# Attention steps of a hybrid trunk layer: five steps an item, three units between scores and transposes, and three norm sums two units later

## The chip, the cores and the metric

One Trainium2 chip, one core. The metric is the time of the kernel on the device in microseconds; the profile beside it shows one execution. PE is TensorE (with PEld for its weight loads), DVE VectorE, ACT ScalarE, SP the engine that issues most DMAs.

## The reference

One layer on h = [16 meta tokens; 512 tokens], width 1024, in float32:

```python
h = h + 0.5 * swiglu(rmsnorm(h, ffn1_norm), w_gate, w_up, w_down)
z = rmsnorm(h, mix_norm) @ w_in
y_rwkv = rwkv7_mix(z[..., :RWKV_COLS], ...)        # 8 heads x 64, state over tokens
y_attn = swa_sink_attention(z[..., RWKV_COLS:] + b_attn, sinks)   # 8 q / 2 kv heads x 64
h = h + concat([y_rwkv, y_attn]) @ w_out
h = h + 0.5 * swiglu(rmsnorm(h, ffn2_norm), ...)
return rmsnorm(h, final_norm)[:, 16:]
```

Attention is causal by chunks of 64 tokens: the queries of a chunk see the 16 meta tokens, their own chunk and the two before it, with a distance penalty and a sink in the softmax:

```python
s = einsum(q, k) * scale - slope * distance      # window and meta columns
p = softmax(concat([sink, s_meta, s_window]))
o = p_meta @ v_meta + p_window @ v_window
```

## The kernel before

The tokens are worked in two halves, hf 0 (272 with the meta tokens) and hf 1 (256). All large products run over weight *units* of 128 x 1024 weights: SP loads `raw`, ACT casts it to `whi` (L124), DVE makes `wlo` = raw − whi (L127), and PE does 24 matmuls of 256 or 272 columns (three products: hi·hi, hi·lo, lo·hi). `drive` walks a list of some 320 units: FFN 1 of both halves, W_in of half 0, W_out of half 0, W_in of half 1, FFN 2 of half 0 with W_out of half 1 in it, FFN 2 of half 1.

Beside the units run two *sides*, which are generators: `rwkv` (`tinv`, the inverse of triangular 32 x 32 blocks in 31 DVE steps L731/L733, closed by DMAs issued on ACT, L739 to L751; then `chain` over the chunks) and `attention`. After each unit `advance` gives each side one step, up to its next `yield UNIT_END`. So a `yield` is a distance of one unit in the program. The order of each engine's instructions is then set by a scheduler with priorities (the chain's instructions rank before their place in the program), so that work of a step can move by a unit or two. Each engine runs its instructions in that order.

In a step of the chain, X1 (L819, L821), X2 (L834) and X3 (L843, L844) are products on PE; between them ACT and DVE copy operands (`Rs` L824, `UV` L836), `values` makes the next chunk's operands in a pair of PSUM banks called `as` (L797, L802; copies L805, L806), and `group_norm` takes sums (L876), a root (L878, with a table load on ACT) and a reciprocal (L879). Attention uses the same single pair `as`. Each half has 4 chunks (`ci`) with 2 *items* (`mp2`, each two query heads on both kv heads), 8 items a half, counted here 1 to 16. An item: scores on PE (L914), maxima on DVE (L920 to L924), exp on ACT with a table load (L927), reciprocals (L929) and scaling (L930), transposes on PE (L935, L937), copies `pT` (L942, L944), products with the values (L947, L950), output as hi and lo parts (L955, L956). Once for each chunk the values are transposed into `VK` (L904 to L908).

Norms: `last(hf)` starts the sum of squares on PE (L315), root and reciprocal (L319, L320) and the split in hi and lo (L345 to L347) of the next layer part's operand. It is called by `drive` from a list `late`: an entry (n, g) waits for n further units before g runs.

Of the kernel before, what the change touches and what calls it, by code (L numbers as in the profile page):

```python
# [37 lines left out]
UNIT_END = -1.0  # L38
# [32 lines left out]
class Prog:  # L71
# [23 lines left out]
    def t(self, pool, shape, tag, dt=F32, bufs=1):  # L95
        return pool.tile(shape, dt, name=self.nm(tag), tag=tag, bufs=bufs)
# [372 lines left out]
    def w_out(self, hf, mo, last):  # L469
        c0 = RO[hf]  # L470

        def f(d):
            def f_(w):
                ps = self.bank()
                self.mm3([ps[:, :256]], w, [lambda k: mo[k // 4][:, k % 4]], 8, WO)
                r = self.res[hf, d][:, c0:TT[hf]]
                self.V.tensor_tensor(out=r, in0=ps[:, :256], in1=r, op=ALU.add)
                self.sq_acc(hf, d, c0)
                if d == NK - 1:
                    self.late.append((0, lambda: last(hf)))  # L480
            return f_

        return [(("o", d), 8, self.cost((hf,), 8), f(d)) for d in range(NK)]
# [405 lines left out]
    def attention(self, hf, st, mo, ap_):  # L889
        A, V, P, PE, t = self.A, self.V, self.P, self.PE, self.t  # L890
        for ci in range(4):
            c = 4 * hf + ci
            nw = min(c + 1, 3)
            W = 17 + 64 * nw
            if c < 3:
                KC, VC = self.KT[:, 0:W], self.VT[:, 0:W]
            else:
                KC, VC = t(ap_, [128, 209], "KC"), t(ap_, [128, 209], "VC")
                for dst, src in ((KC, self.KT), (VC, self.VT)):
                    P.tensor_copy(out=dst[:, 0:17], in_=src[:, 0:17])  # L900
                    P.tensor_copy(out=dst[:, 17:], in_=src[:, 17 + 64 * (c - 2):17 + 64 * (c + 1)])
            VK = t(ap_, [128, 2, 128], "VK")
            b = self.banks()[0]
            PE.transpose(b[0:81, 0:128], VC[:, 0:81], self.ident)  # L904
            if nw > 1:
                PE.transpose(b[0:W - 81, 128:256], VC[:, 81:W], self.ident)
                A.copy(out=VK[0:W - 81, 1], in_=b[0:W - 81, 128:256])
            A.copy(out=VK[0:81, 0], in_=b[0:81, 0:128])  # L908
            yield UNIT_END
            kss = (slice(0, 64), slice(64, 128))  # L910
            for mp2 in range(2):
                bs, rows = self.banks(), []
                for b, ks in zip(bs, kss):
                    PE.matmul(b[:, 0:W], st["Q"][ks, ci, 2 * mp2:2 * mp2 + 2, :].rearrange("p m t -> p (m t)"), KC[ks, 0:W],  # L914
                              start=True, stop=True)
                for kv in range(2):
                    g, x = 2 * kv + mp2, bs[kv][:, 0:W]
                    s = t(ap_, [128, 209], "s", bufs=2)
                    m = t(ap_, [128, 4], "m", bufs=4)
                    V.tensor_tensor_reduce(out=s[:, 0:17], in0=x[:, 0:17], in1=self.tabm[:, g, c], scale=1.0, scalar=-3e38,  # L920
                                           op0=ALU.add, op1=ALU.max, accum_out=m[:, 0:1])
                    V.tensor_tensor_reduce(out=s[:, 17:W], in0=x[:, 17:W], in1=self.tabw[:, g, 192 - 64 * nw:], scale=1.0,
                                           scalar=-3e38, op0=ALU.add, op1=ALU.max, accum_out=m[:, 1:2])
                    V.tensor_scalar(out=m[:, 2:3], in0=m[:, 0:1], scalar1=m[:, 1:2], scalar2=-1.0, op0=ALU.max, op1=ALU.mult)  # L924
                    rows.append((s, m))
                for s, m in rows:
                    A.activation(s[:, 0:W], s[:, 0:W], AF.Exp, bias=m[:, 2:3], accum_out=m[:, 3:4])  # L927
                for s, m in rows:
                    V.reciprocal(m[:, 3:4], m[:, 3:4])  # L929
                    A.activation(s[:, 0:W], s[:, 0:W], AF.Copy, scale=m[:, 3:4])  # L930
                yield UNIT_END
                yield UNIT_END
                b, bo = self.banks()
                for kv, (s, m) in enumerate(rows):
                    PE.transpose(b[0:81, 256 * kv:256 * kv + 128], s[:, 0:81], self.ident)  # L935
                    if nw > 1:
                        PE.transpose(b[0:W - 81, 256 * kv + 128:256 * kv + 256], s[:, 81:W], self.ident)  # L937
                yield UNIT_END
                pTs = []
                for kv in range(2):  # L940
                    pT = t(ap_, [128, 2, 128], "pT", bufs=2)
                    A.copy(out=pT[0:81, 0], in_=b[0:81, 256 * kv:256 * kv + 128])  # L942
                    if nw > 1:
                        A.copy(out=pT[0:W - 81, 1], in_=b[0:W - 81, 256 * kv + 128:256 * kv + 256])  # L944
                    pTs.append(pT)
                for kv, ks in enumerate(kss):
                    PE.matmul(bo[ks, 0:128], VK[0:81, 0, ks], pTs[kv][0:81, 0], start=True, stop=(nw == 1))  # L947
                if nw > 1:
                    for kv, ks in enumerate(kss):
                        PE.matmul(bo[ks, 0:128], VK[0:W - 81, 1, ks], pTs[kv][0:W - 81, 1], start=False, stop=True)  # L950
                yield UNIT_END
                ms, ts = slice(2 * mp2, 2 * mp2 + 2), slice(64 * ci, 64 * ci + 64)
                ov = bo[:, 0:128].rearrange("p (m t) -> p m t", m=2)
                mh, ml = mo[1][:, ms, 0, ts], mo[1][:, ms, 1, ts]
                A.copy(out=mh, in_=ov)  # L955
                V.tensor_tensor(out=ml, in0=ov, in1=mh.bitcast(F32), op=ALU.subtract)  # L956
                yield UNIT_END


def program(tc, io, out):  # L960
    with ExitStack() as ctx:
        pr = Prog(ctx, tc, io)
        n = {}
        A, B, AB = (0,), (1,), (0, 1)
# [6 lines left out]
        def final(hf):  # L971
# [6 lines left out]
            for d in (0, 1, 2, 3, 6, 7, 4, 5):  # L978
# [6 lines left out]
                if d % 2:  # L985
# [1 line left out]

        gu = lambda f, g, hfs: pr.ffn_gu(f, g, hfs, n)
        dn = lambda f, g, hfs, last=None: pr.ffn_down(f, g, hfs, last, last is final and hfs == B,
                                                           6 if last is final and hfs == A else 0)  # L990
        act = lambda fn: [(None, 0, 0, fn)]
        pools = {}

# [215 lines left out]
```

## Time and the profile before

| what | value |
|---|---|
| median of 3 runs | 1140.03 us (1139.44 to 1143.7) |
| the profiled execution | 1143.3 us, its span 1140.5 us |
| PE busy | 1084.7 us, 95% |
| DVE busy | 826.8 us, 72% |
| ACT busy | 674.6 us, 59% |

The span runs from the first to the last instruction that the profiler saw; the time of the same execution holds 2.8 us more. Busy shares are means over the whole span, whose stages have different limits.

### The profile page before, as it was taken

The page shows a single profiled execution, that of the slowest core. Times are in us where ns is not written, and L with a number is a line of the kernel's source. Part 1 is how long each engine was busy: PE and PEld are TensorE (multiplying, and loading weights), DVE is VectorE, ACT ScalarE, POOL GpSimd, SP SyncE. Part 2 cuts the span into 40 slices and gives each one's busy share as a digit, 9 for nine tenths or more (in the row PEclk, how much of TensorE's full clock was granted, in tenths as well). Part 3 has the DMA queues.
Part 4 walks back from the last instruction along what each step waited for, and adds up shares of the span by engine and source line. Part 5 has one row for each costly group of instructions (what it writes and reads, how often), then busy time and mean ns, then how long its engine had stood idle before and what let it go on. Part 6 is the DMA issues. An engine that isn't in the chain of part 4 may idle for free.

```text
span 1140.5 us, 23845 instructions
## 1 busy us (share of the span) xinstructions
PE 1084.7 (95%) x9621; PEld 1022.1 (90%) x9621; DVE 826.8 (72%) x1533; ACT 674.6 (59%) x1166; POOL 31.6 (3%) x91
## 2 busy tenths in 40 slices
PE   8999999999999997989999998998999899999996
PEld 7999999998899997878989898997888898888884
DVE  7866666777778994466888776995676488776666
ACT  7545454676667634676667685563667477545453
POOL 0000000021000000000001000000000000000000
PEclk8999999999999998999999998997999899999998
DMA  7565655544336546222655445546225356666661
GB/s 267 181 183 170 202 171 166 184 146 152 126 115 198 173 147 172 95 66 86 182 152 169 144 137 164 153 145 188 76 76 167 108 158 201 212 209 187 188 193 60
DMA packets 68722, 178.82 MB, mean 157 GB/s; under 512 B 21620, under 2 KB 26868, under 8 KB 68612
## 3 DMA queue, kind: packets, MB, share of 16 engines
q1 hardware_dynamic: 52384, 173.70, 49.5%
q10 hardware_dynamic: 16228, 3.61, 1.5%
q8 instruction: 75, 1.23, 0.4%
q14 instruction: 35, 0.29, 0.1%
HBM read 173.54 MB, written 3.74 MB: 155 GB/s over the span
## 4 chain that ended last, share of the span: by engine, by line
PE 79%; DVE 8%; ACT 6%; DMA 3%; issue 3%; ACTq 1%; DVEq 0%; SPq 0%
PE big L218 19%; PE big L219 18%; PE big L200 13%; PE big L206 11%; PE big L208 5%; PE big L227 5%; DVE wlo L127 2%; ACT whi L124 2%; DVE tmp L731 2%; DVE rn L733 1%; DMA zk<-d 1%; ACT s L927 1%; PE as L914 1%; DMA d<-rn 1%; ACT L927 1%
## 5 line engine op out<-in xcount | busy, mean ns | idle before, releaser
L124 ACT CAST whi<-raw 128x1024 fp32r<-128x1024 f32 (+1 forms) x321 | 334.5, 1044 | 289.8 <-PE big L219 150.1
L127 DVE TENSOR_TENSOR wlo<-raw,whi 128x1024 fp32r<-128x1024 f32 x320 | 389.5, 1218 | 112.6 <-ACT whi L124 93.4
L218 PE MATMUL big<-n0a,whi 128*128 128x272 f32 (+1 forms) x464 | 124.0, 296 | 10.0 <-ACT whi L124 5.7
L219 PE MATMUL big<-h,whi 128*128 128x256 f32 (+1 forms) x528 | 133.0, 285 | 0.0
L218 PE MATMUL big<-h,whi 128*128 128x256 f32 (+1 forms) x528 | 130.8, 286 | 1.4 <-ACT whi L124 1.4
L219 PE MATMUL big<-n0a,whi 128*128 128x272 f32 (+1 forms) x464 | 122.4, 292 | 0.4 <-DVE n0a L347 0.3
L218 PE MATMUL big<-n0b,whi 128*128 128x272 f32 (+1 forms) x464 | 121.7, 293 | 0.8 <-ACT n0b L955 0.4
L219 PE MATMUL big<-n0b,whi 128*128 128x272 f32 (+1 forms) x464 | 121.3, 291 | 0.4 <-DVE n0b L347 0.4
L218 PEld LDWEIGHTS big<-h,whi 128*128 128x128 f32 x528 | 98.5, 189 | 2.8 <-ACT whi L124 1.6
L218 PEld LDWEIGHTS big<-n0a,whi 128*128 128x128 f32 x464 | 89.8, 194 | 12.1 <-ACT whi L124 6.8
L219 PEld LDWEIGHTS big<-h,whi 128*128 128x128 f32 x528 | 99.3, 189 | 1.3 <-issue 0.9
L219 PEld LDWEIGHTS big<-n0a,whi 128*128 128x128 f32 x464 | 90.1, 194 | 1.8 <-DVE n0a L347 0.9
L218 PEld LDWEIGHTS big<-n0b,whi 128*128 128x128 f32 x464 | 89.4, 194 | 2.3 <-ACT n0b L346 0.9
L219 PEld LDWEIGHTS big<-n0b,whi 128*128 128x128 f32 x464 | 89.3, 193 | 1.4 <-DVE n0b L347 0.7
L218 PE MATMUL big<-n1a,whi 128*128 128x256 f32 x288 | 76.6, 295 | 6.9 <-ACT whi L124 6.3
L227 PE MATMUL big<-h,wlo 128*128 128x256 f32 (+1 forms) x528 | 78.6, 284 | 0.4 <-DVE wlo L127 0.4
L200 PE MATMUL big<-n0b,wlo 128*128 128x272 f32 (+1 forms) x464 | 77.6, 288 | 0.0
L200 PE MATMUL big<-n0a,wlo 128*128 128x272 f32 (+1 forms) x464 | 77.0, 288 | 0.0
L218 PE MATMUL big<-n1b,whi 128*128 128x256 f32 x288 | 76.1, 295 | 0.7 <-ACT n1b L955 0.7
L219 PE MATMUL big<-n1b,whi 128*128 128x256 f32 x288 | 76.2, 294 | 0.0
L219 PE MATMUL big<-n1a,whi 128*128 128x256 f32 x288 | 76.1, 293 | 0.0
L227 PEld LDWEIGHTS big<-h,wlo 128*128 128x128 f32 x528 | 69.7, 188 | 1.5 <-issue 0.8
(313 smaller groups left out, 2218.6 us busy)
## 6 DMA issues: line engine op xcount, KB each, us to landing
raw<-w_in SPq DMA_DIRECT2D x319, 512.0 KB, 3.7
outT<-o SPq DMA_DIRECT2D x8, 256.0 KB, 2.6
res<-xT_in SPq DMA_DIRECT2D x2, 544.0 KB, 5.1
res<-xT_in SPq DMA_DIRECT2D x2, 512.0 KB, 8.7
d<-GT ACTq DMA_DIRECT2D x8, 80.0 KB, 3.5
zk<-d ACTq DMA_DIRECT2D x2, 320.0 KB, 5.0
d<-rn ACTq DMA_DIRECT2D x2, 320.0 KB, 3.5
GT<-d ACTq DMA_DIRECT2D x8, 80.0 KB, 6.2
```

Source lines behind the costliest of these rows:

```text
L124: self.A.copy(out=hi[:, a:a + n], in_=raw[:, a:a + n])
L127: self.V.tensor_tensor(out=lo[:, 0:nk], in0=raw[:, 0:nk], in1=hi[:, 0:nk].bitcast(F32), op=ALU.subtract)
L200: self.PE.matmul(o, lo[:, k], x(k)[:, 0], start=False, stop=(k == ks[-1]))
L206: self.PE.matmul(o, hi[:, i], x(k).rearrange("p a t -> p (a t)"), start=(k == first), stop=False)
L208: self.PE.matmul(o[:, 0:256], lo[:, i], x(k)[:, 0], start=False, stop=(k == last))
L218: self.PE.matmul(o, w, x[:, 0], start=first, stop=False)
L219: self.PE.matmul(o, w, x[:, 1], start=False, stop=False)
L227: self.PE.matmul(o, lo[:, i], x(k)[:, 0], start=False, stop=(k == nk - 1))
L731: V.tensor_tensor(out=m, in0=NT[:n2, 0:k, k].unsqueeze(1).broadcast_to([n2, k, k]), in1=TI[:n2, 0:k, 0:k], op=ALU.mult)
L733: V.tensor_reduce(out=TI[:n2, 0:k, k], in_=m, op=ALU.add, axis=mybir.AxisListType.X)
L914: PE.matmul(b[:, 0:W], st["Q"][ks, ci, 2 * mp2:2 * mp2 + 2, :].rearrange("p m t -> p (m t)"), KC[ks, 0:W], start=True, stop=True)
L927: A.activation(s[:, 0:W], s[:, 0:W], AF.Exp, bias=m[:, 2:3], accum_out=m[:, 3:4])
```

## The change

Attention, for each item: before, the value transposes of a chunk were a step of their own, and an item then had the steps scores, nothing, transposes, product, output: 11 steps a chunk. After, the value transposes stand in the first item's transpose step (in another part of the bank `bo`), the output stands in the product's step, and two steps with nothing follow the scores' step: 5 steps an item, 10 a chunk, with three units between scores and transposes in place of two. The norm that W_out starts goes from 0 to 2 further units, and so does the one that FFN 1's last W_down of half 1 starts. Lines of attention have a number lower by 7 (scores L907, maxima L913 to L917, exp L920, reciprocals L922, scaling L923), transposes are L934 and L936, `VK` L928 to L932, `pT` L941 and L943, products L946 and L949, output L953.

```diff
                 if d == NK - 1:
-                    self.late.append((0, lambda: last(hf)))
+                    self.late.append((2, lambda: last(hf)))
...
             VK = t(ap_, [128, 2, 128], "VK")
-            b = self.banks()[0]
-            PE.transpose(b[0:81, 0:128], VC[:, 0:81], self.ident)
-            if nw > 1:
-                PE.transpose(b[0:W - 81, 128:256], VC[:, 81:W], self.ident)
-                A.copy(out=VK[0:W - 81, 1], in_=b[0:W - 81, 128:256])
-            A.copy(out=VK[0:81, 0], in_=b[0:81, 0:128])
-            yield UNIT_END
...
                     A.activation(s[:, 0:W], s[:, 0:W], AF.Copy, scale=m[:, 3:4])
-                yield UNIT_END
-                yield UNIT_END
+                for _ in range(3):
+                    yield UNIT_END
                 b, bo = self.banks()
+                if mp2 == 0:
+                    PE.transpose(bo[0:81, 128:256], VC[:, 0:81], self.ident)
+                    if nw > 1:
+                        PE.transpose(bo[0:W - 81, 256:384], VC[:, 81:W], self.ident)
+                        A.copy(out=VK[0:W - 81, 1], in_=bo[0:W - 81, 256:384])
+                    A.copy(out=VK[0:81, 0], in_=bo[0:81, 128:256])
...
                         PE.matmul(bo[ks, 0:128], VK[0:W - 81, 1, ks], pTs[kv][0:W - 81, 1], start=False, stop=True)
-                yield UNIT_END
                 ms, ts = slice(2 * mp2, 2 * mp2 + 2), slice(64 * ci, 64 * ci + 64)
...
-                                                           6 if last is final and hfs == A else 0)
+                                                           6 if last is final and hfs == A else 2 if f == 1 and hfs == B else 0)
```

How the change moves instructions, at three places. On ACT at item 6 (half 0, second item of its third chunk), from the item's table load on, before:

```order
L927 ACT_TABLE_LOAD
L927 ACTIVATE s_5606,m_5607<-s_5606,m_5607 128x209
L927 ACTIVATE s_5611,m_5612<-s_5611,m_5612 128x209
L124 CAST whi_6530<-raw_6529 128x1024
L930 ACTIVATE s_5606<-s_5606,m_5607 128x209
L930 ACTIVATE s_5611<-s_5611,m_5612 128x209
L400 ACT_TABLE_LOAD
L400 ACTIVATE silu_6592<-big_6535 128x256
L824 COPY Rs_5677<-mx_5659 128x256
L942 COPY pT_5820<-as_5730 81x128
```

and after:

```order
L920 ACT_TABLE_LOAD
L920 ACTIVATE s_5381,m_5382<-s_5381,m_5382 128x209
L920 ACTIVATE s_5386,m_5387<-s_5386,m_5387 128x209
L824 COPY Rs_5446<-mx_5428 128x256
L923 ACTIVATE s_5381<-s_5381,m_5382 128x209
L923 ACTIVATE s_5386<-s_5386,m_5387 128x209
L878 ACT_TABLE_LOAD
L878 ACTIVATE grs_5490<-mx_5488,dv 128x256
L836 COPY UV_5245<-mx_5493 64x256
L805 COPY UV_5504<-as_5506 64x256
L806 COPY BT_5505<-as_5506 128x256
```

After, X2's operand `Rs` of the chain, a group norm's root and the chain's copies of `UV` and `BT` stand behind this item's exps and scalings; the cast of weights that stood between exps and scalings stands ahead of the item.

On DVE at item 9 (half 1, first item) and the first steps of the half's inverse (L731, L733), before:

```order
L127 TENSOR_TENSOR wlo_8796<-raw_8794,whi_8795 128x1024
L731 TENSOR_TENSOR tmp_8149<-zk_8144,rn_8146 80x1
L733 TENSOR_REDUCE rn_8146<-tmp_8149 80x1
L731 TENSOR_TENSOR tmp_8149<-zk_8144,rn_8146 80x4
L401 TENSOR_TENSOR silu_8875<-big_8849,silu_8875 128x256
L733 TENSOR_REDUCE rn_8146<-tmp_8149 80x2
L127 TENSOR_TENSOR wlo_8845<-raw_8843,whi_8844 128x1024
L731 TENSOR_TENSOR tmp_8149<-zk_8144,rn_8146 80x9
L403 TENSOR_TENSOR h_1333_8874<-silu_8875,h_1333_8874 128x256
L733 TENSOR_REDUCE rn_8146<-tmp_8149 80x3
L920 ISA s_8437,m_8438<-as_8434,tabm 128x17
```

and after:

```order
L915 ISA m_8393 128x1
L127 TENSOR_TENSOR wlo_8866<-raw_8864,whi_8865 128x1024
L401 TENSOR_TENSOR silu_8896<-big_8870,silu_8896 128x256
L917 TENSOR_SCALAR m_8388<-m_8388 128x1
L917 TENSOR_SCALAR m_8393<-m_8393 128x1
L731 TENSOR_TENSOR tmp_8145<-zk_8140,rn_8142 80x1
L733 TENSOR_REDUCE rn_8142<-tmp_8145 80x1
L731 TENSOR_TENSOR tmp_8145<-zk_8140,rn_8142 80x4
L127 TENSOR_TENSOR wlo_8903<-raw_8901,whi_8902 128x1024
L733 TENSOR_REDUCE rn_8142<-tmp_8145 80x2
L403 TENSOR_TENSOR h_1336_8895<-silu_8896,h_1336_8895 128x256
L922 RECIPROCAL m_8388<-m_8388 128x1
```

The item's maxima, which stood behind the inverse's third step, now stand ahead of its first; the reciprocals (L922) stand behind its second.

On ACT at the end of half 1's attention, items 15 and 16, from the last copy of item 15's transposed probabilities, before:

```order
L944 COPY pT_10523<-as_10478 128x128
L402 CAST h_1652_11158<-silu_11159 128x256
L955 CAST n1b_8102<-as_10478 128x2x64
L927 ACT_TABLE_LOAD
L927 ACTIVATE s_10603,m_10604<-s_10603,m_10604 128x209
L927 ACTIVATE s_10608,m_10609<-s_10608,m_10609 128x209
L930 ACTIVATE s_10603<-s_10603,m_10604 128x209
L930 ACTIVATE s_10608<-s_10608,m_10609 128x209
```

and after:

```order
L943 COPY pT_10410<-as_10367 128x128
L402 CAST h_1634_11082<-silu_11083 128x256
L124 CAST whi_11089<-raw_11088 128x1024
L400 ACTIVATE silu_11151<-big_11094 128x256
L953 CAST n1b_8098<-as_10367 128x2x64
L124 CAST whi_11120<-raw_11119 128x1024
L402 CAST h_1644_11150<-silu_11151 128x256
L920 ACT_TABLE_LOAD
L920 ACTIVATE s_10459,m_10460<-s_10459,m_10460 128x209
L920 ACTIVATE s_10464,m_10465<-s_10464,m_10465 128x209
L923 ACTIVATE s_10459<-s_10459,m_10460 128x209
L923 ACTIVATE s_10464<-s_10464,m_10465 128x209
```

Item 15's output and item 16's table load now have casts of weights and a silu before each.

## Rows read from the trace of the kernel before

**Rows 1.** The page's first part: busy us (share of the span), instructions.

```profile
PE 1084.7 (95%) x9621; PEld 1022.1 (90%) x9621; DVE 826.8 (72%) x1533; ACT 674.6 (59%) x1166; POOL 31.6 (3%) x91
```

**Rows 2.** PE's waits: waiting line, releaser: us in total, times, longest us.

```profile
PE big L218 <- ACT whi L124: 13.4, 3, 6.3
PE as L935 <- ACT s L930: 8.0, 3, 3.6
PE mx L843 <- ACT grs L878: 4.7, 3, 2.5
PE mx L844 <- DVE UV L836: 3.3, 5, 1.4
PE big L315 <- DVE acc L310: 2.7, 2, 2.5
PE as L947 <- ACT pT L944: 2.6, 2, 1.8
```

**Rows 3.** Windows: us, busy of PE, PEld, DVE, ACT, POOL (count), PEclk, DMA, GB/s.

```profile
509.24:516.06 6.82, 5.85 (x26) 5.68 (x27) 1.65 (x2) 5.11 (x12) 0.00 (x0) 0.50 0.26 77
881.29:884.70 3.41, 3.41 (x16) 2.63 (x14) 1.08 (x10) 0.90 (x1) 0.00 (x0) 0.50 0.50 154
697.89:776.06 78.17, 74.61 (x648) 72.52 (x648) 75.21 (x149) 45.11 (x80) 1.06 (x4) 0.96 0.50 152
```

**Rows 4.** Timelines of PE and ACT at item 6: start, us, instruction [idle before].

```profile
504.07 0.62 PE L914 MATMUL as<-KT,Q 64*128 64x209 f32 x4
506.54 1.28 ACT L927 ACT_TABLE_LOAD   x1
510.20 0.50 PE L935 MATMUL as<-ident,s 128*81 128x128 f32 x1 [2.78 <-ACT s L930]
```

**Rows 5.** Timelines of ACT and PE beside item 13, in the chain.

```profile
829.88 1.28 ACT L927 ACT_TABLE_LOAD   x1
832.20 1.28 ACT L878 ACT_TABLE_LOAD   x1
833.87 0.35 ACT L836 COPY UV<-mx 64x256 f32<-64x256 f32 x1
834.12 0.83 ACT L930 ACTIVATE s<-s,m 128x209 f32<-128x209 f32 x2
835.90 0.37 ACT L806 COPY BT<-as 128x256 f32<-128x256 f32 x1
834.03 0.27 PE L843 MATMUL mx<-UV,BT 64*64 64x64 f32 x1 [2.05 <-ACT grs L878]
834.15 0.57 PE L843 MATMUL mx<-UV,BT 64*64 64x64 f32 x13
```

**Rows 6.** Timelines of DVE, PE and ACT: item 9 and the inverse's end.

```profile
697.89 0.16 DVE L731 TENSOR_TENSOR tmp<-zk,rn 80x1 f32<-80x1 f32 x1 [5.38 <-DMA zk<-d]
704.59 0.50 PE L935 MATMUL as<-ident,s 128*81 128x128 f32 x1 [3.56 <-ACT s L930]
784.77 1.04 ACT L124 CAST whi<-raw 128x1024 fp32r<-128x1024 f32 x1 [9.19 <-DMA zk<-d]
```

**Rows 7.** Timeline of PE at items 15 and 16.

```profile
879.94 0.44 PE L947 MATMUL as<-pT,VK 81*64 81x128 f32 x4 [1.75 <-ACT pT L944]
886.53 0.34 PE L935 MATMUL as<-ident,s 128*81 128x128 f32 x1 [1.64 <-ACT s L930]
```

**Rows 8.** Timelines of DVE and PE at the norms, halves 1 and 0.

```profile
575.84 0.48 DVE L347 SCALAR_TENSOR_TENSOR n1b<-sq,pv,n1b 128x256 fp32r<-128x256 f32 x1
579.59 0.28 PE L218 MATMUL big<-n1a,whi 128*128 128x256 f32 x1
585.13 0.70 PE L315 MATMUL big<-acc,ones 128*128 128x256 f32 x2 [2.50 <-DVE acc L310]
```

**Rows 9.** Groups by line: busy, mean ns | idle before, releasers.

```profile
L127 DVE TENSOR_TENSOR wlo<-raw,whi 128x1024 fp32r<-128x1024 f32 x320 | 389.5, 1218 | 112.6 <-ACT whi L124 93.4
```

## The prediction

> **What bounds the kernel now.** I read the page first, then the list of PE's waits, then the clock by stretches, then the timelines of the stretches that the change moves. The page [rows 1] shows PE busy for 95% of the span, DVE 72%: the multiplication of weights sets the time, and only what interrupts it can be won. The list of waits [rows 2] says what does. The casts of weights (L124) hold PE 13.4 us in 3 places, attention's transposes (L935) wait 8.0 us in 3 places for the softmax's last scaling (L930), the chain's third step (L843, L844) waits 4.7 and 3.3 us, a norm's sum (L315) 2.7, the product with the values (L947) 2.6. Behind some waits the granted clock stands at 0.50, the lower of TensorE's two levels (1.2 and 2.4 GHz) [rows 3]: after the wait of 2.78 us at 510 us, and after that of 1.75 us at 880 us. PE was busy 5.85 us in the first such window and 3.41 in the second, so each cost half of that, 2.9 and 1.7 us.
>
> A unit is 24 matmuls. In the last window of [rows 3] 648 matmuls keep PE busy 74.61 us: 0.115 us each, 2.76 a unit. In that window, the second half's triangular inverse, DVE is busy 75.21 of 78.17 us: there DVE is the bound, not PE.
>
> **The change part by part.** All positions are from the order of the instructions, all durations from the trace of before. No arithmetic is added; one activation table load more is.
>
> *Item 6 (510 us).* Before, the scores start at 504.07, the table load for exp at 506.54 (2.47 later), and the transposes at 510.20 after a wait of 2.78 [rows 4]. Removing that wait and the window behind it gives 2.78 + 2.9 = 5.7. But the place is not empty afterwards. Between scores and transposes now stand the chain's first product, `values`, a group norm's sum, and the chain's second and third products (X2, X3), and the ACT steps that feed these stand behind this item's table load and exps. From the table load to the end of two exps is 832.20 − 829.88 = 2.32; two scalings (L930) 0.83; the group norm's table load and root 833.87 − 832.20 = 1.67; a copy 0.37, four of them 1.3 [rows 5] (833.87 is the start of the copy of UV). ACT then has X2's operand at 2.47 + 2.32 + 0.37 = 5.2 us after the scores, and DVE's addition takes about another 0.4 (taken like the copy). PE comes to X2 after 9 weight matmuls (1.0) and about 43 small ones at 0.57 / 13 = 0.044 (1.9): at 2.9. New wait: 5.6 − 2.9 = 2.7. X3's operand comes at 5.2 + 0.83 + 1.67 + 0.37 = 8.0, PE is there at 7.0: 1.0 more. The bank pair for the transposes is free after four more copies, at 9.3; PE is there at 8.9: 0.4. So 4.1 comes back of 5.7, and **1.6** stays. The bounds: +5.7 if ACT's copies find room, −1.3 if the new wait of 2.7 brings a window at half clock (2.9) of its own.
>
> Here the Trainium skill (ScalarE: Activation LUTs, What ACT_TABLE_LOAD costs) speaks against the change: a switch is about 1283 ns of load and about 1380 ns of drain, 2.66 us. By it the path through two loads would be up to 2.8 us longer and this item would lose 1.2. The trace has 1.28 us for the load [rows 4, 5], with no idle time of ACT shown before it, so the sum goes by 1.28; the same holds for the one load that is new, which lies on ACT beside other work.
>
> *Chain beside item 13 (834 us).* Before, X3 waits 2.05 us there for the root L878 [rows 5] behind the same table load and exps. Now two casts of weights, both scalings and a load for silu stand ahead of it as well, some 3.5 us of ACT, while PE has 33 weight matmuls (3.8) more to do before it gets there. I take **−1.0**; bounds +2 and −4.
>
> *Item 9 and the second half's inverse (690 to 787 us).* Before, DVE's first inverse step (L731) stands ahead of item 9's score work, waits 5.38 us for a DMA, and the transposes wait 3.56 us [rows 6]. Now the score work stands ahead of L731, but the two reciprocals of the softmax stand behind it, so a part of the wait stays. What counts is when the inverse ends, since ACT then issues a row of DMAs and the next cast is 9.19 us late [rows 6]. The change puts the last gram products 1.25 units later (3.45 us) and one more unit's DVE work inside: 1.22 for the lower halves of the weights [rows 9] and two small products like the 0.37 copies, 2.0 in all. Of DVE's idle 2.96 us in that window I take 2.2 as caused by item 9's wait, and gone. So the inverse ends 3.45 + 2.0 − 2.2 = 3.2 later, and PE has done two units (5.5) more by then (the casts in front of the DMA issue are 221, not 219): gain **2.3**, bounds 0 and 5.
>
> *The second half's tail (878 to 890 us).* Item 15's transposes come two units earlier, and its product with the values one unit: 34 weight matmuls (3.9 us) now lie between the two, where a wait of 1.75 us was [rows 7]. Item 16 stays about where it was, its scores 10 matmuls before its transposes, so its 1.64 stays. Gain 1.75 + half of the window's 1.7: **2.6**, bounds 1 (the next wait takes its place) and 4.
>
> *Norms.* The sum after the first half's W_out waits 2.50 us for DVE's last addition [rows 8]; two units later that addition is long done, and what the sum feeds (the second FFN's input) is used only after W_in of the other half. Against it: the second half's mixing norm now starts three units (8.3 us) later. Its split ends at 576.3 now [rows 8] and would end near 584.6, while W_in's first unit starts to read it at 579.6 [rows 8]; part `a` of the split comes first, and three units' `a` halves now run ahead of their `b` halves. I take 1.5 of loss: **+1.0**, bounds +2.5 and −3.
>
> *Value transposes, and the output in one step with the product.* The two transposes and two copies of each chunk move three units later and still come before their use; they cost nothing as long as ACT reaches the copies before the transposed probabilities. The output's cast on ACT now stands directly behind the product that it waits for, with the next cast of weights queued behind it. With new small waits at items 7, 8 and 14 I take **−1.0**; bounds 0 and −3.
>
> Sum: 1.6 − 1.0 + 2.3 + 2.6 + 1.0 − 1.0 = 5.5 us off. The rows are of an execution of 1143.3 us (span 1140.5 and 2.8 around it), so 1137.8 on its scale; the median of before is 3.3 below that execution, so **1134.5**. A measurement of this kernel tells 0.5% (5.7 us) from no change, so this stands on the edge.
>
> **The rivals.**
> *Slower: the chain waits in order.* X2 and X3 stand ahead of all weights on PE, and their operands stand behind softmax, roots and casts on ACT, all with table loads. For it: 8.0 us are lost so already, and item 6 now puts softmax between X1 and X2. If each of the eight chunks waits the longest of [rows 2], 2.5, that is 20 against 8.0 now, where the sum has 5 us of growth (the 4.1 and 1.0): 7 more, and two windows at half clock (3.4 each) another 7: **1148**. It decides once these waits grow by 5 + 5.5 + 5.7 = 16 us. Against it: two of the 2-us waits of now had no such window behind them. A sentence beside it: the Trainium skill (PSUM — Partial Sum Buffer, Engine vs sequencer instructions) has the queues of ScalarE and VectorE as strict FIFO, and the trace agrees where L731's wait of 5.38 holds the score work behind it; more distance on PE then brings nothing where the late step is queued behind another.
>
> *The gain is given back.* Item 6's new wait brings its own half clock (−2.9), and the inverse's end moves as much as PE does (−2.3): 0.3 is left, **1140**. For it: DVE is saturated in that window whatever PE does; against it: the tail and the norm do not depend on either.
>
> *More: the waits go and none comes.* 8.0 + 2.6 + 2.5 + windows of 2.9 and 1.7 = 17.7: **1122**. Against it: the reciprocals behind L731, and item 16's unchanged distance.
>
> **How the numbers follow.** The sum as worked out 0.50 (own range 1129 to 1140), given back 0.20, more 0.14, slower 0.16. From them: faster by over 0.5% is 0.32 of the first and nearly all of "more", 0.45; within 0.5% the rest of the first and of "given back", 0.39; slower 0.16. The range 1122 to 1143 leaves out nearly all of the slower case and a part of "more".
>
> **What would show it.** Right: no wait of L934 (the transposes) above 1 us at item 6, but waits at L834 and L843 there; PE's cast wait at the end of the second inverse after 788 us and about as long; item 15's product without a wait, item 16's transposes with about 1.6; L315 of W_out without a wait. Wrong: L834/L843/L844 with over 16 us, or W_in's first units waiting for the split (L346, L347) by over 3 us, or an inverse that ends as early as before.

## The result, and the profile after

The changed kernel takes 1129.55 us (median of 4 runs, 1126.56 to 1132.82) against 1139.74 of before (4 runs): a ratio of 0.9905 with a 95% interval of 0.9885 to 0.9925, so 10.2 us off. Forecast were 5.5 us. The sign and the range held, the size did not: the sum let the chain's waits grow by some 5 us, and they fell by some 6. One execution of e13 below, of 1477.78 us at a granted clock of 0.65, is in no median and no ratio.

The page of the changed kernel, its span and its first line, as in [rows 1]:

```profile
span 1124.5 us, 23829 instructions
PE 1080.1 (96%) x9621; PEld 1016.9 (90%) x9621; DVE 824.9 (73%) x1533; ACT 675.3 (60%) x1167; POOL 36.1 (3%) x91
```

The span is 16.0 us shorter than the other one (these two executions lie at opposite ends of their runs, which is why it is more than 10.2). PE's busy time falls by 4.6 us, its idle time by 11.4 (55.8 to 44.4), with the same 9621 matmuls. PE's waits of the changed kernel, to be read against [rows 2]:

```profile
PE big L218 <- ACT whi L124: 6.0, 1, 6.0
PE as L934 <- ACT s L923: 6.0, 4, 2.1
PE mx L759 <- DMA zk<-d: 4.7, 1, 4.7
PE as L946 <- ACT pT L943: 1.5, 2, 0.8
PE mx L876 <- ACT Rs L824: 1.1, 1, 1.1
PE mx L843 <- ACT grs L878: 0.4, 1, 0.4
PE mx L844 <- DVE UV L836: 0.3, 1, 0.3
```

L843 and L844, the chain's third step, went from 4.7 and 3.3 us to 0.4 and 0.3, where the prediction had them grow; new is 1.1 us at L876. The transposes (L934 now) went only from 8.0 to 6.0. The cast wait after the inverse of half 1 became a wait of the first product of its end (L759), 4.7.

Where the time went by halves can be read from two windows that hold the same work, from the start of unit 188 (before half 1's attention) to that of unit 240 (behind it): before, and then after; columns as in [rows 3].

```profile
678.89:902.14 223.25, 204.72 (x2260) 192.97 (x2259) 156.70 (x329) 125.39 (x246) 4.53 (x16) 0.93 0.45 132
```

```profile
671.44:886.13 214.69, 200.92 (x2260) 188.51 (x2259) 156.74 (x331) 125.91 (x248) 6.67 (x16) 0.96 0.47 137
```

Both have 2260 matmuls. The stretch is 8.6 us shorter: 4.8 us less idle PE (18.5 to 13.8) and 3.8 us less busy PE at a mean granted clock of 0.96 in place of 0.93. From the start of unit 132 to that of 152, half 0's chain, before took 103.5 us and the changed kernel 98.3 in these two executions, a gain that the experiments below don't find again in the medians. The stretch between the two, from unit 152 to 188, where the norms lie, went from 124.4 to 121.9 us.

Item 6 and item 9, and the tail, on PE's timeline of the changed kernel, against [rows 4], [rows 6] and [rows 7]:

```profile
492.91 0.62 PE L907 MATMUL as<-KT,Q 64*128 64x209 f32 x4
497.93 0.70 PE L876 MATMUL mx<-gsq,bones 128*128 128x256 f32 x2 [1.08 <-ACT Rs L824]
498.74 0.46 PE L834 MATMUL mx<-Rs,GT 64*64 64x64 f32 x10
500.68 0.68 PE L843 MATMUL mx<-UV,BT 64*64 64x64 f32 x16
502.01 0.34 PE L934 MATMUL as<-ident,s 128*81 128x128 f32 x1
521.26 0.34 PE L934 MATMUL as<-ident,s 128*81 128x128 f32 x1 [1.91 <-ACT s L923]
696.20 0.34 PE L934 MATMUL as<-ident,s 128*81 128x128 f32 x1 [1.52 <-ACT s L923]
870.96 0.34 PE L934 MATMUL as<-ident,s 128*81 128x128 f32 x1 [2.08 <-ACT s L923]
872.89 0.69 PE L946 MATMUL as<-pT,VK 81*64 81x128 f32 x4 [0.85 <-ACT pT L943]
```

At item 6 the wait of 2.78 is gone and one of 1.08 stands before X2 (in the sum: 2.7), none before X3 at 500.68 (1.0) and none before the transposes at 502.01 (0.4); item 7's transposes (521.26) now wait 1.91. Item 9 still waits 1.52 of its 3.56, since the reciprocals stand behind the inverse's first steps, as the order said. Item 16 still waits 2.08 and 0.85.

### The profile page after: what moved, and what is told of

It is laid out like the page before. It is cut to its first block, busy times and chain, and to the rows that moved or that the text cites. A ratio compares the mean times of both kernels' runs of the same rounds, so it can differ in the third digit from the quotient of the medians.

```text
span 1124.5 us, 23829 instructions
## 1 busy us (share of the span) xinstructions
PE 1080.1 (96%) x9621; PEld 1016.9 (90%) x9621; DVE 824.9 (73%) x1533; ACT 675.3 (60%) x1167; POOL 36.1 (3%) x91
## 4 chain that ended last, share of the span: by engine, by line
PE 72%; DVE 13%; ACT 7%; issue 3%; DMA 3%; ACTq 1%; DVEq 0%; SPq 0%
PE big L218 17%; PE big L219 16%; PE big L200 12%; PE big L206 11%; PE big L208 5%; DVE wlo L127 4%; PE big L227 4%; DVE tmp L731 3%; DVE rn L733 2%; ACT whi L124 2%; DMA zk<-d 1%; DMA d<-GT 1%; ACT s L920 1%; ACT L400 1%; DVE res L446 1%
## 5 line engine op out<-in xcount | busy, mean ns | idle before, releaser
L219 PE MATMUL big<-h,whi 128*128 128x256 f32 (+1 forms) x528 | 135.4, 289 | 0.0
L218 PE MATMUL big<-h,whi 128*128 128x256 f32 (+1 forms) x528 | 131.9, 288 | 0.9 <-ACT silu L400 0.9
L218 PE MATMUL big<-n0a,whi 128*128 128x272 f32 (+1 forms) x464 | 122.3, 293 | 4.3 <-ACT n0a L346 2.3
L219 PE MATMUL big<-n0a,whi 128*128 128x272 f32 (+1 forms) x464 | 120.6, 289 | 0.4 <-DVE n0a L347 0.3
L218 PE MATMUL big<-n0b,whi 128*128 128x272 f32 (+1 forms) x464 | 120.4, 290 | 0.4 <-ACT n0b L346 0.3
L219 PE MATMUL big<-n0b,whi 128*128 128x272 f32 (+1 forms) x464 | 120.1, 289 | 0.4 <-DVE n0b L347 0.4
L219 PEld LDWEIGHTS big<-h,whi 128*128 128x128 f32 x528 | 101.1, 192 | 1.6 <-issue 1.3
L218 PEld LDWEIGHTS big<-h,whi 128*128 128x128 f32 x528 | 100.4, 193 | 1.3 <-ACT silu L400 1.1
L218 PEld LDWEIGHTS big<-n0a,whi 128*128 128x128 f32 x464 | 88.1, 190 | 6.8 <-ACT n0a L346 2.5
L219 PEld LDWEIGHTS big<-n0b,whi 128*128 128x128 f32 x464 | 88.1, 190 | 2.0 <-DVE n0b L347 0.7
L219 PEld LDWEIGHTS big<-n0a,whi 128*128 128x128 f32 x464 | 88.3, 191 | 1.6 <-DVE n0a L347 0.9
L218 PEld LDWEIGHTS big<-n0b,whi 128*128 128x128 f32 x464 | 88.0, 191 | 1.5 <-ACT n0b L346 0.9
L218 PE MATMUL big<-n1b,whi 128*128 128x256 f32 x288 | 73.9, 289 | 0.4 <-ACT n1b L953 0.4
L219 PE MATMUL big<-n1b,whi 128*128 128x256 f32 x288 | 73.9, 288 | 0.0
```

What stands on the lines that cost most here:

```text
L218: self.PE.matmul(o, w, x[:, 0], start=first, stop=False)
L219: self.PE.matmul(o, w, x[:, 1], start=False, stop=False)
```

## The experiments

All medians are of 4 to 12 runs; each ratio is to the kernel before on the same chip, with its 95% interval. Gains "by the ratio" are that share of the time of before. e3 to e8, e10 to e12 and e16 have the new norms, e9 and e13 to e15 the old ones.

**1. The two parts apart.** e1 is the changed kernel with the two `late` entries put back, e2 the kernel before with them alone:

```diff
# e1_attn_only, on the changed kernel
-self.late.append((2, lambda: last(hf)))
+self.late.append((0, lambda: last(hf)))
...
-6 if last is final and hfs == A else 2 if f == 1 and hfs == B else 0)
+6 if last is final and hfs == A else 0)
```

> Attention's part of the change alone, all three norms as before. Theory A (the gain is attention's: the chain's waits of 8.0 us and the half-clock windows behind waits go): 7 to 9 us below before, some 1132; the wait of 2.5 us at W_out's L315 is there again. Theory B (the norms carry half or more, since the two profiles part by 1.7 and 2.9 us at the two norms of the middle): only 4 to 6 us below before, 1135.

> The norms' part alone, attention as before. Theory A: 1 to 3 us below before (the one wait of 2.5 us), 1138; the transposes' waits of 8.0 us, the chain's of 8.0 us and the half-clock windows at 510, 704 and 881 us stay. Theory B: 4 to 6 us below before, 1135.

Measured: e1 1130.82 us, 0.9923 (0.9899 to 0.9947); e2 1138.78 us, 0.9988 (0.9973 to 1.0004). Theory A holds: the gain is attention's, the norms alone give 1.4 us by the ratio, at most 3.1 by the interval. The wait of 2.5 us is there again in e1, one instruction ahead of L315: 2.71 us at L572.

**2. Distance or phase.** On the changed kernel:

```diff
# e3_gap2
-                for _ in range(3):
+                for _ in range(2):
                     yield UNIT_END
# e4_shift1, ahead of attention's first loop
+        yield UNIT_END
         for ci in range(4):
```

> The changed kernel with two units in place of three between scores and transposes, so four steps an item. Theory C (distance: three units are what softmax needs): 3 to 6 us above the changed kernel, the transposes wait 8 us or more in all (6.0 us in the changed kernel). Theory D (phase: what counts is where an item's exps fall against the chain's steps of three a chunk): the transposes' waits change little, the chain's waits at L843, L844 and L876 (1.8 us in the changed kernel) go up by 4 us or more or not at all, as the new phase has it.

> The changed kernel with one empty step ahead of each half's attention, so every item comes one unit later against the chain, the distance of three kept. Theory C: within 2 us of the changed kernel, waits of the transposes about 6 us. Theory D: the chain's waits return, 4 us or more at L843, L844 and L876, and the time is 3 us or more above the changed kernel's.

Measured: e3 1121.83 us, 0.9840 (0.9815 to 0.9865), 7.7 us *below* the changed kernel; e4 1132.27 us, 0.9935 (0.9914 to 0.9956), 2.7 above it. Theory C falls: two units are better than three, and with them the transposes wait less, not more (2.3 us against 6.0). These are PE's waits in e3:

```profile
PE mx L759 <- DMA zk<-d: 3.6, 1, 3.6
PE mx L844 <- DVE UV L836: 3.0, 5, 1.1
PE as L934 <- ACT s L923: 2.3, 2, 1.7
```

Theory D has e4's waits on its side (L876 and L844, the chain's second and third steps, wait 8.3 us there), but not e3, whose chain waits more at L844 than the changed kernel's and which still is faster. So a third theory was formed: what counts is how many steps attention takes.

**3. The number of steps.** e5 is the changed kernel with one unit of distance (six steps a chunk); e6 has two units and the output in a step of its own (ten); e7 two units and the value transposes in a step of their own (nine); e8 two units and an empty step behind the output (ten):

```diff
# e8_gap2_pad
-                for _ in range(3):
+                for _ in range(2):
                     yield UNIT_END
...
                 V.tensor_tensor(out=ml, in0=ov, in1=mh.bitcast(F32), op=ALU.subtract)
                 yield UNIT_END
+                yield UNIT_END
```

> The changed kernel with one unit between scores and transposes: three steps an item, six a chunk (the change has ten, two units gave eight and 1121.8 us). Theory E (the number of steps decides: the sooner attention is through, the fewer items stand in the tail of half 1): at or below 1122 us, the tail after 860 us without waits. Theory F (two units are the least that softmax needs): the transposes wait for L923 10 us or more, 1130 us or above.

> The value transposes in the first item's step, but the output a step of its own again and two units of distance: ten steps a chunk, as in the change, and the new norms. Theory E: the count of steps is the change's, so 1128 to 1132 us. Theory H (each merging has its price, since the pair of banks is held through a step of its own): the output still holds the pair a unit longer, 1125 to 1135, with waits of the chain's values (L797) for the output.

> The output in the product's step, but the value transposes a step of their own again and two units of distance: nine steps a chunk, and the new norms. Theory E: between eight steps (1121.8) and ten (1129.6), so 1124 to 1128 us. Theory H: the value transposes' own step costs four times a round trip through the pair, 1128 us or more.

> Two units of distance, and the unit that was taken out put behind the item's output instead: ten steps a chunk as in the change, nothing else moved. Theory E: as the change, 1128 to 1132 us. Theory I (it is the third unit between scores and transposes itself that costs, by what the chain then puts between): 1120 to 1124 us, as with eight steps.

Measured, by steps a chunk. The column "ahead" counts on PE's timelines the items whose scores come before the chain's first `values`, in half 0 and in half 1 (numbered on from half 0's eight as 9 to 16, so 12 means items 9 to 12); section 4 needs it.

| steps a chunk | kernel | ahead | median us | ratio (95% interval) |
|---|---|---|---|---|
| 11 | e2 (old steps, new norms) | 3, 11 | 1138.78 | 0.9988 (0.9973 to 1.0004) |
| 10 | e4 (changed, one empty step ahead of attention) | 3, 11 | 1132.27 | 0.9935 (0.9914 to 0.9956) |
| 10 | changed | 4, 12 | 1129.55 | 0.9905 (0.9885 to 0.9925) |
| 10 | e6 | 4, 12 | 1127.11 | 0.9884 (0.9866 to 0.9903) |
| 10 | e8 | 4, 12 | 1127.47 | 0.9885 (0.9867 to 0.9904) |
| 9 | e7 | 4, 12 | 1128.54 | 0.9902 (0.9884 to 0.9919) |
| 8 | e3 | 4, 12 | 1121.83 | 0.9840 (0.9815 to 0.9865) |
| 6 | e5 | 6, 14 | 1119.92 | 0.9828 (0.9807 to 0.9849) |

Theory E comes out for e5's time, though not for its tail, where a cast of the last group norm (L885) holds PE 4.2 us; e6 and e8 lie up to 1 us below its range, and F and I fall. The changed kernel, e6 and e8, with ten steps, lie within 2.5 us wherever the tenth step stands: in front of the transposes, of the output, or behind it. So the third unit between scores and transposes buys nothing by itself. The count is not all: e4 has ten steps as well and lies 2.7 us above the changed kernel, and e7, with nine, should lie between eight and ten and does not. For e7, theory H (a price of the value transposes' own step) and the column "ahead", in which e7 is like the kernels with ten steps, both fit; no run parts them. In e3 item 4's and item 12's transposes come ahead too, not only their scores.

**4. A candidate for why fewer steps win: who takes the pair first.** The chain's first `values` take the bank pair while the inverse is still running and hold it until the copies out of it run (from 799.56 us on in half 1 of before, behind the copy L769 of the inverse's last product on ACT); attention stands still meanwhile. Before: the values at 758.15, their copies at 799.56, and item 12's scores only at 803.66.

```profile
758.15 0.51 PE L797 MATMUL as<-cent,vT 64*64 64x64 f32 x10
798.96 0.57 ACT L769 COPY GT<-mx 32x512 f32<-32x512 f32 x1 [0.99 <-PE mx L767]
799.56 0.37 ACT L805 COPY UV<-as 64x256 f32<-64x256 f32 x1
803.66 0.62 PE L914 MATMUL as<-KC,Q 64*128 64x209 f32 x2
```

After the change item 12's scores stand ahead of the values, at 740.65:

```profile
740.65 0.62 PE L907 MATMUL as<-KC,Q 64*128 64x209 f32 x4
745.99 0.51 PE L797 MATMUL as<-cent,vT 64*64 64x64 f32 x10
802.47 0.34 PE L934 MATMUL as<-ident,s 128*81 128x128 f32 x1
```

One softmax fewer then meets the chain. The same can be had with the old steps, if the chain comes later in the program:

```diff
# e9_old_late_chain on the kernel before, e10_new_late_chain on the changed one
                 pclose("ti")
+                for _ in range(4):
+                    yield UNIT_END
                 cp = popen("ch")
```

e11 has the new steps in half 0 and the old ones in half 1, e12 the other way round, both with the new norms.

> The kernel before with its old steps and old norms, and four empty steps between the inverse and the chain in the program, so that the chain's first values take the bank pair after items 4 and 12 have come through and not before (in the order: scores and transposes of item 4 at units 118.6 and 122.2, values at 125.4, where before it was values at 118.6, then item 4 at 133.1). Theory J (the change's gain is that item 4 and item 12 pass before the chain takes the pair for the length of the inverse, so that one item fewer a half meets the chain and the tail): 7 to 12 us below before, 1128 to 1133, with no waits of item 16's kind in the tail. Theory K (it is the steps themselves, the transposes of the values and the output held apart): within 3 us of before.

> The changed kernel with the same four empty steps ahead of the chain: item 4 and item 12 come through whole before the pair is taken (in the changed kernel only their scores do). Theory J: 3 to 7 us below the changed kernel, 1122 to 1127. Theory K: within 2 us of it.

> The new attention steps in half 0 alone, half 1 with the old ones, the new norms. If the gain is even by halves as the two profiles part (about 5 us in half 0's chain stage, 8.6 in half 1's, 16 in all): 4 to 5 us below before, 1135. By the prediction's terms (1.6 for item 6 and little else in half 0): 1137 to 1139.

> The new attention steps in half 1 alone, half 0 with the old ones, the new norms. By the profiles: 6 to 8 us below before, 1132 to 1134. By the prediction's terms (2.3 for the inverse, 2.6 for the tail, 1.0 lost beside item 13): 3 to 5 us below, 1135 to 1137.

Measured: e9 1124.50 us, 0.9878 (0.9852 to 0.9903): the old steps and the old norms with a later chain do at least as well as the change. e10 1113.84 us, 0.9776 (0.9752 to 0.9801), 15.7 us below the changed kernel. e11 1139.74 us, 1.0008 (0.9984 to 1.0031): half 0, with the new norms, gives nothing that can be measured. e12 1130.11 us, 0.9919 (0.9898 to 0.9941), below both of its forecasts: half 1, with the new norms, gives about the whole gain. Theory J's two kernels came out faster than it said; by halves it does not hold evenly, since half 0's item 4 also passes its scores ahead of the hold in e11.

e4 bears on theory J too. There the values come first again and item 12's scores wait behind the hold:

```profile
742.97 0.51 PE L797 MATMUL as<-cent,vT 64*64 64x64 f32 x10
799.83 0.62 PE L908 MATMUL as<-KC,Q 64*128 64x209 f32 x4
```

Neither item 4 nor item 12 passes in e4, and it still gains 0.65%, against 0.12% of e2, whose items stand the same and whose steps are the old ones. So the new steps gain some 0.5% with no item passing, and passing can be only part of the change's 0.95%; how large a part is not shown, since e4 also moves every item by a unit against the chain.

**5. Which place of half 1.** e13 and e14 put two and four empty steps ahead of the chain in half 1 alone, on the kernel before (`for _ in range(2 * (hf == 1))`); e15 has the new steps for half 1's first chunk alone; e16 is e3 with four empty steps ahead of the chain.

> The kernel before, with two empty steps ahead of the chain in half 1 alone: as in the changed kernel, item 12's scores come before the chain takes the pair and its transposes after; item 16's scores and transposes stay in the tail (units 235.6 and 236.5). If passing ahead of the chain's hold is what pays in half 1: 6 to 9 us below before, 1130 to 1133. If it is the tail or item 9: within 3 us of before.

> The kernel before, with four empty steps ahead of the chain in half 1 alone: item 12 passes whole, and item 16's transposes come at unit 234.6, ahead of where W_out waits for them. If the tail pays: 4 us or more below e13. If the hold pays: within 3 us of e13.

> The kernel before, with the new steps in half 1's first chunk alone (items 9 and 10): item 9's scores come two units earlier, ahead of the inverse's first step on DVE; item 12 stays behind the hold and item 16 in the tail. If item 9's wait with its window at half clock pays: 3 to 6 us below before. If not: within 2 us.

> The changed kernel with two units of distance (eight steps a chunk, 1121.8 us) and four empty steps ahead of the chain (which took the changed kernel to 1113.8 us). If both work through the same thing, the items that meet the chain: 1111 to 1115 us, no sum of the two. If they are separate gains: 1104 to 1108 us.

Measured: e13 1129.49 us (median of five runs), 0.9915 (0.9899 to 0.9931); e14 1133.92 us, 0.9945 (0.9928 to 0.9961); e15 1133.68 us, 0.9958 (0.9943 to 0.9972); e16 1116.51 us, 0.9797 (0.9780 to 0.9815).

e13 moves item 12's scores ahead of the hold as the change does, keeps the waits of item 16, and gains as much as the change:

```profile
755.99 0.62 PE L914 MATMUL as<-KC,Q 64*128 64x209 f32 x4
760.62 0.51 PE L797 MATMUL as<-cent,vT 64*64 64x64 f32 x10
874.10 0.34 PE L935 MATMUL as<-ident,s 128*81 128x128 f32 x1 [1.82 <-ACT s L930]
875.75 0.44 PE L947 MATMUL as<-pT,VK 81*64 81x128 f32 x4 [0.85 <-ACT pT L944]
```

But it moves more than that: all of half 1's chain starts two units later against items 13 to 16. Before, X3 waits 2.0 us (L843) and 2.3 us (L844) in the window of units 188 to 240, and item 15's product 1.75 [rows 7]; in e13 these waits are gone. These two lines of before's waits in that window, and all of e13's:

```profile
PE mx L844 <- DVE UV L836: 2.3, 3, 1.4
PE mx L843 <- ACT grs L878: 2.0, 1, 2.0
```

```profile
PE as L935 <- ACT s L930: 5.0, 2, 3.2
PE mx L759 <- DMA zk<-d: 4.7, 1, 4.7
PE as L947 <- ACT pT L944: 0.8, 1, 0.8
PE big L218 <- ACT whi L124: 0.6, 1, 0.6
PE big L218 <- ACT n1b L955: 0.4, 1, 0.4
```

So e13 shows that the place of the chain in half 1 is worth as much as the change, and not whether passing the hold or the chain's place beside the later items pays. The same window of units 188 to 240, in e13 and then in e15:

```profile
678.50:888.44 209.94, 198.38 (x2260) 187.39 (x2259) 156.45 (x329) 126.85 (x247) 7.98 (x16) 0.97 0.48 140
```

```profile
678.50:891.77 213.27, 198.00 (x2260) 186.33 (x2259) 155.90 (x329) 121.78 (x244) 5.74 (x16) 0.97 0.46 138
```

Both have less idle time and a higher mean clock (0.97 against 0.93) than before over the same 2260 matmuls. In e14 the waits of the tail are gone as well, and by the ratios it is 0.30% (3.4 us) slower than e13, outside both of its forecasts; a wait of 2.98 us for X2's operand stands at 811.14 us instead. What the tail gives may be lost again there; the profile of e14 is of its fastest run (1129.80) and can't show it.

e15 gains 0.42%, some 4.8 us, with item 12 behind the hold, about half of the change's gain; in it item 9's wait of 3.56 us and the window at half clock behind it are gone. They are gone in e2 too, where item 9's transposes wait 0.30 us; yet e2 gains 0.12% in all, and its window of units 188 to 240 is about as long as before's:

```profile
674.10:896.74 222.64, 200.01 (x2260) 186.85 (x2259) 157.30 (x331) 131.44 (x252) 9.96 (x16) 0.95 0.45 132
```

So what is won at item 9 need not last to the end of the half. e13's gain and e15's don't add up: the change has both places and gains what e13 gains alone. Nor do e3's and e10's: e16 lies above e10, and above both of its forecasts.

## Why the prediction was wrong

**The chain's waits: the step that failed.** The sum let the waits of X2 and X3 grow by some 5 us, 4.1 at item 6 and 1.0 beside item 13. In the trace they fell by 6.2: L843 and L844 from 8.0 to 0.7, with 1.1 new at L876.

*Chain beside item 13 (−1.0)* had the wrong sign. It took the third X3 of half 1, which waited 2.05 us [rows 5], to keep a softmax and its casts ahead of its root. In the changed kernel the items meet other steps of the chain. The third X3 is the one at 827.53; item 13's exps (from 816.45) stand 9 us ahead of its root (825.40), and it does not wait. The order with both scalings and a load for silu ahead of the root belongs to item 14 and the fourth X3, and that waits 0.38:

```profile
816.45 0.47 ACT L920 ACTIVATE s<-s,m 128x209 f32<-128x209 f32 x1 [3.52 <-DVE m L917]
825.40 0.47 ACT L878 ACTIVATE grs<-mx,dv 128x256 f32<-128x256 f32 x1
827.53 0.68 PE L843 MATMUL mx<-UV,BT 64*64 64x64 f32 x16
842.06 0.68 PE L843 MATMUL mx<-UV,BT 64*64 64x64 f32 x16 [0.38 <-ACT grs L878]
844.30 0.68 PE L844 MATMUL mx<-UV,BT 64*64 64x64 f32 x16
```

All waits of half 1's X3 went from 4.3 us to 0.7, a gain of 3.6 where the sum had a loss of 1.0. The −1.0 did not follow from its own working either: 3.5 us more on ACT against 3.8 more on PE leave no new wait. For half 1 as a whole the sum had 3.9 us (−1.0 + 2.3 + 2.6); e12 less the norms (e2) gives 0.69%, 7.9 us. How that divides between the chain's waits, item 9 and item 12's passing stays open, as said above.

**Item 9 and the inverse (2.3).** The mechanism came as worked out: counted from the start of unit 188 the inverse's last step on DVE ends 2.3 us later than before (3.2 in the working), and PE has done 47 more weight matmuls by the end of its wait behind it (two units in the working). That part of item 9's wait stays (1.52 us) was right too. Left out of the sum was the window at half clock behind that wait (703.80 to 710.62), which the changed kernel does not have. e15 gives 4.8 us, but it moves item 10 as well and shortens half 1's X3 waits from 4.3 to 3.0 us.

**Item 6 (1.6).** Not found in the medians: e11, with the new norms, gives 1.0008, and e2, with these norms alone, 0.9988. The wait of 2.78 went, and 1.08 at X2 and 1.91 at item 7's transposes came, which leaves nothing of it. The other 2.9 of the term was the window at half clock behind the wait. In e13, whose half 0 has the steps of before, the same transposes wait 2.79 us at 510.14, and the stretch of [rows 3] is at full clock:

```profile
510.14 0.34 PE L935 MATMUL as<-ident,s 128*81 128x128 f32 x1 [2.79 <-ACT s L930]
509.24:516.06 6.82, 5.91 (x60) 5.49 (x61) 1.88 (x3) 6.76 (x15) 0.00 (x0) 1.00 0.23 77
```

Of the profiles with this same wait, before has 6.8 us at 0.50 behind it, e14 has 3.4, and e2, e12, e13 and e15 have none. So the window does not follow from the wait alone, and a sum can't count on winning it back.

**The tail (2.6).** Over-sized: item 15's wait is gone, item 16's is longer, and a window at 0.50 from 871.19 to 878.02 lies behind it. The waits from item 15's product on were 1.75, 0.36, 1.64, 0.85 and 0.36 and are 2.08, 0.85 and 0.36, 1.7 us less; no run has the tail alone.

**Norms (1.0).** Right by the medians: e2 has 1.4 us. The sum after W_out (L315) starts without a wait, and the loss that was feared at W_in did not come. In the traces the stretch of units 152 to 188 is 2.5 us shorter in the changed kernel and 2.9 in e2 (121.5 us), so the term was rather too small at its place.

**The table load's drain.** By an estimate from the Trainium skill's 2.66 us (ScalarE: Activation LUTs, What ACT_TABLE_LOAD costs) X2 at item 6 should have come later by 1.4 than by the rows; the wait was shorter than by the rows, so the trace does not show the longer price (the exp starts at 496.61, 1.29 after its load at 495.32).

**The rivals.** The chain's in-order waits (1148) did not come: they fell from 8.0 us to 0.7 (1.8 with L876). "More" (1122) had the right direction for those waits but took the transposes' waits as gone too, and they were not.

What stays open: why item 9's place and the chain's later start do not add, why scores alone ahead of the hold pay in half 1 (if it is they that pay) and not in half 0, and why the new steps gain in e4 without any item passing. The gains lie in the same stretch, in idle time and in time at half clock, and the windows of half clock do not come back behind the same wait, as at item 6, so that the profile of one execution can't settle it.

## What to carry to other kernels

When two strands share one buffer pair, look at who holds it through the other's long wait, and try the start of one strand a few units later first: two empty steps ahead of the chain in half 1 were worth as much as the whole rewriting of the steps, though not shown to be by the buffer alone. When a change shifts two strands against each other, work out anew which step meets which. A longer distance between producer and consumer is no gain by itself where every step also costs a turn: count the turns. And price a moved step by the stretch that it leaves as well as by the one that it enters.

## What was not expected of the hardware

Kernels with many waits differ from run to run by 4 to 13 us (e11: 1133.02 to 1146.23), and e10 (4 runs), whose profile has only one window of 10.24 and one of 3.41 us at a granted clock of 0.50 between 330 and 900 us, by 0.3 us (1113.76 to 1114.03). These are its two windows:

```profile
437.44:447.68 10.24, 9.03 (x93) 8.45 (x94) 5.62 (x7) 5.62 (x8) 0.00 (x0) 0.50 0.54 173
775.36:778.77 3.41, 3.39 (x18) 3.17 (x20) 3.41 (x4) 2.82 (x5) 0.00 (x0) 0.50 0.29 63
```

In the profile of before there are 44 us of such windows in the same stretch, in that of the changed kernel 24. So the fastest kernel here was also the steadiest; that the windows cause the scatter is what these numbers suggest, and the window at item 6 that one execution has and another lacks, not what a run here isolates.
